# Reordering single steps: the first half's output projection and row norm against the second half's attention and convolution norm

## The chip, the cores and the metric

The kernel runs on one core of a Trainium2 chip. The metric is the device time of one execution in microseconds; lower is better. All data is float32. Matrix products are made three times over (high part by high part, high by low, low by high), each operand being split into a rounded high part and the rest.

## The reference

One hybrid decoder layer on 1024 tokens of 1024 channels. What matters here:

```python
proj = x @ w_in + b_in                       # q 512, k 128, v 128, a 512, gate 512 columns
y_attn = sliding_window_gqa(q, k, v, sinks, rel_bias_table)   # 8 heads, blocks of 128, own and previous block
h = causal_depthwise_conv(a * sigmoid(gate), conv_dw_w, conv_dw_b)      # 31 taps
y_conv = silu(layer_norm(h, conv_ln_g, conv_ln_b))
y = concat([rms_norm(y_attn, attn_out_gain), rms_norm(y_conv, conv_out_gain)])
x = layer_norm(ALPHA * x + y @ w_out + b_out, ln1_g, ln1_b)
h = causal_depthwise_conv(x @ w_up, ffn_dw_w, ffn_dw_b)       # 3 taps, 5632 columns
g, u = split(h)
out = layer_norm(ALPHA * x + (silu(g) * u) @ w_down, ln2_g, ln2_b)
```

## The kernel before

The 1024 tokens are two halves of 512, H = 0 and H = 1, each of four tiles of 128 tokens. Every stage is a Python generator that issues some instructions and yields. A string, `SCRIPT`, says in which order the generators are advanced: one letter, one step. The letters that matter here:

- `o`, `out_proj(0)`: the output projection of the first half, four steps, one for each 256 output columns. A step casts and splits its weights (L231 on ScalarE, L233 on GpSimd), makes 96 matmuls (L638 to L644) and adds them to the residual rows (`acc`, L648 and L650 on VectorE). `O` is the same for the second half.
- `l`, `first_norm` with `ln1(0)`: four steps, one for each token tile: row statistics (L298, L300), the power on GpSimd (L293), three operations on a row of 1024 (L311 VectorE, L312 GpSimd, L313 VectorE), eight transposes (L278), their copies (L281 ScalarE, L282 VectorE). `L` is the same for the second half, to which `other_sums` (L747) adds the block sums that the later product needs.
- `A`, `attn(1)`: the attention of the second half. 16 units (a token tile, a key group, a pair of heads) go through `front` (six score matmuls L505, L510 on VectorE, L517 the exponential on ScalarE, L526 on GpSimd), then one step later `mid` (four transposes L537, a copy L539, a subtraction L540), then one step later `back` (six matmuls L558 to L560; after every fourth unit L565 and L567), and after a tile its sum (L578). That makes 21 steps. `a` is the same for the first half.
- `C`, `conv(1)`: the 31-tap convolution of the second half on VectorE (L421). `N`, `conv_norm(1)`: the norm of its result, three steps: sums on GpSimd (L443, L444), a matmul (L445), subtractions (L449), squares and their sums (L433); then the reciprocal deviation spread by a matmul (L459, L461); then scaling, SiLU and the gains (L466 to L472).
- `f`, `ffn(0, alone)`: the first six of 22 channel groups of the feed-forward part for the first half. Nine steps: up, up, down, three times. An up step is two products of 24 matmuls (L265, L266, L268) with their convolution (L673 to L678) and gate (L691 to L694); a down step is 48 matmuls (L713 to L715), added by L720. It needs all four `l` steps.
- `s`, `first_sums`: sums of the first half's columns. After the script comes `joint`, the rest of the feed-forward part on both halves at once (from L793 on).

The letters set the order in which instructions are written down. A planner then places each engine's instructions by that order and by the time at which it expects their data, so an instruction written later can stand ahead on its engine. Matrix products that were tied together (`chain`), taps and loads keep their written order. On the chip each engine works through its own list in order.

SBUF places are fixed by hand in lanes that several tiles use in turn. Three of these orders matter: the convolution norm of the second half uses lanes 40 to 47, which hold the first half's attention output until `out_proj(0)` has read it; the second half's output projection keeps its weights in lanes 48 to 55, which hold the second half's values (`vpad`) and transposed probabilities (`ph`) until attention's last `back`; and `ln1(0)` writes to lanes 16 to 31, which hold `out_proj(0)`'s weights.

```python
LANES_NORM1 = {'nsum': [44, 45], 'nz': [40], 'nsq': [42, 43, 46, 47]}
LANES_OUT1 = {'bo': [32], 'oh': [48, 49, 50, 51, 52], 'ol': [53, 54, 55, 38, 39], 'or': [34, 36]}
    for k in SCRIPT:
        if k == 'c':
            drain(steps[k])
        else:
            next(steps[k], None)
    drain(*steps.values())
```

Of the kernel before, what the change touches and what calls it, by code (L numbers as in the profile page):

```python
# [33 lines left out]
LINE = 384  # L34
GROUP = 2
ALONE = 6
SCRIPT = ('0hx00j0hxixxiiiggacaaaaaaaaaaaaannnCCaaagagCkCqqaaaqqoAAAoA'
          'AAAAoAAoNAlAlNAlAlNAAAAfAfAAOOOfsOsssffLLLLffff')
SKEW = (1, 2, 5)
KOFF = (4, 5)  # L40
AHEAD = 1
# [28 lines left out]
def hybrid_layer_kernel(  # L70
# [132 lines left out]
    def parameters():  # L203
        tp = psB()
        for i, pr in enumerate((pr1, pr2, pr3)):
            nc.tensor.transpose(out=tp[:, i * P:(i + 1) * P], in_=pr, identity=ident)
        nc.vector.tensor_copy(out=par, in_=tp[:, 0:3 * P].rearrange("p (i c) -> p i c", c=P))
        nc.vector.tensor_scalar(out=bq8, in0=par[:, 0, 0:4], scalar1=-0.125, scalar2=None, op0=ALU.mult)
# [799 lines left out]
    parameters()  # L1008
    for k in SCRIPT:
        if k == 'c':  # L1010
# [63 lines left out]
```

## Time and profile before

| | |
|---|---|
| median of three runs | 1112.66 us (1112.2 to 1114.48) |
| profiled execution | 1113.39 us |
| its span, first to last instruction | 1111.6 us |
| mean granted TensorE clock | 0.981 |
| TensorE matmul busy | 1050.4 us, 94% |
| VectorE busy | 788.9 us, 71% |
| ScalarE busy | 481.9 us, 43% |
| GpSimd busy | 654.5 us, 59% |

A row of the windows view gives, for a stretch of the span, its length, then for each engine the busy time in it and the number of instructions, then the granted TensorE clock and the DMA share. A row of the timeline has start, duration, engine, line, operation, the tiles it writes and reads, and in brackets the engine's idle time before it and what ended that. A row of the groups has busy time and mean nanoseconds, then the idle time before.

### The profile page before, as it was taken

To read this page: it belongs to the slowest core of one execution; us is meant where nothing else is said; L and a number is where in the kernel's file an instruction comes from. 1 tells how busy PE (TensorE), PEld (TensorE's weight loads), DVE (VectorE), ACT (ScalarE), POOL (GpSimd) and SP (SyncE) were. 2 spreads that over 40 slices of the span, in tenths; PEclk is the share of its full clock that TensorE was granted. 3 is DMA by queue.
4 is the path that set the end of the run, shared out by engine and by line. 5 is a ranking of instruction groups with operands and counts; after the bars stand their busy time and mean duration, and the time that the engine had idled before them with its cause. 6 is when DMAs were issued, how large, how long until landed. Compare 5 with 4: busy or idle time off the path is not lost.

```text
span 1111.6 us, 14383 instructions
## 1 busy us (share of the span) xinstructions
PE 1050.4 (94%) x5113; PEld 873.9 (79%) x5113; DVE 788.9 (71%) x1430; ACT 481.9 (43%) x915; POOL 654.5 (59%) x560
## 2 busy tenths in 40 slices
PE   7999999878968999898999999999999999999996
PEld 5887778778957998676788787878788787888875
DVE  2899789999897448985746656564747566569656
ACT  4546677753548333462515242433425142442430
POOL 3749688775587556455736372746556363636551
PEclk9999999999978999899999999999999999999999
DMA  6535221413600242131211021111212110233321
GB/s 183 160 87 132 77 57 40 139 53 98 186 20 1 78 132 65 50 110 43 76 37 59 20 82 32 58 56 38 76 39 76 35 60 20 76 114 115 113 95 75
DMA packets 115641, 85.19 MB, mean 77 GB/s; under 512 B 20354, under 2 KB 108017, under 8 KB 115569
## 3 DMA queue, kind: packets, MB, share of 16 engines
q1 hardware_dynamic: 112368, 78.92, 23.9%
q10 hardware_dynamic: 3201, 5.35, 1.4%
q8 instruction: 40, 0.66, 0.2%
q14 instruction: 32, 0.26, 0.1%
HBM read 80.05 MB, written 4.21 MB: 76 GB/s over the span
## 4 chain that ended last, share of the span: by engine, by line
PE 76%; DVE 13%; DMA 4%; POOL 3%; ACT 3%; issue 1%; SPq 0%; POOLq 0%; DVEq 0%; ACTq 0%
PE psA L265 6%; PE psA L266 6%; PE psA L268 5%; PE psS L713 2%; PE psS L714 2%; PE psS L715 2%; PE psS L796 2%; PE psS L794 2%; PE psS L793 2%; PE psA L794 2%; PE psA L796 2%; PE psA L793 2%; PE psS L505 2%; PE psA L638 1%; PE psA L713 1%
## 5 line engine op out<-in xcount | busy, mean ns | idle before, releaser
L233 POOL TENSOR_TENSOR wl<-raw,wh 128x512 fp32r<-128x512 f32 x196 | 263.3, 1355 | 162.2 <-ACT wh L231 68.9
L231 ACT CAST wh<-raw 128x512 fp32r<-128x512 f32 x196 | 119.1, 620 | 173.5 <-PE psA L266 24.1
L233 POOL TENSOR_TENSOR wl<-ts,wh 128x512 fp32r<-128x512 f32 x64 | 82.5, 1296 | 155.4 <-ACT wh L231 135.5
L421 DVE SCALAR_TENSOR_TENSOR psC<-hconv,const,psC 128x512 f32<-128x512 f32 x196 | 147.3, 751 | 3.5
L265 PE MATMUL psA<-x,wh 128*128 128x512 f32 x336 | 135.9, 404 | 7.9 <-DVE z L678 4.1
L266 PE MATMUL psA<-x,wh 128*128 128x512 f32 x336 | 134.4, 400 | 0.0
L231 ACT CAST wh<-ts 128x512 fp32r<-128x512 f32 x64 | 39.3, 622 | 177.4 <-PE psS L715 39.2
L268 PE MATMUL psA<-x,wl 128*128 128x512 f32 x336 | 87.2, 396 | 0.6 <-POOL wl L233 0.6
L265 PEld LDWEIGHTS psA<-x,wh 128*128 128x128 f32 x336 | 64.9, 193 | 23.9 <-issue 4.7
L266 PEld LDWEIGHTS psA<-x,wh 128*128 128x128 f32 x336 | 64.9, 193 | 13.5 <-issue 0.2
L268 PEld LDWEIGHTS psA<-x,wl 128*128 128x128 f32 x336 | 62.3, 188 | 15.1 <-issue 1.2
L293 POOL TENSOR_TENSOR tiny<-tiny,const 128x1 f32<-128x1 f32 (+1 forms) x28 | 26.5, 951 | 53.7 <-DVE tiny L292 50.7
L720 DVE TENSOR_TENSOR acc<-psS,acc 128x512 f32<-128x512 f32 x52 | 35.7, 688 | 31.4 <-PE psS L715 31.4
L233 POOL TENSOR_TENSOR ol<-or,oh 128x512 fp32r<-128x512 f32 x32 | 40.7, 1296 | 18.9 <-ACT oh L231 16.6
L793 PE MATMUL psA<-x,wh 128*128 128x512 f32 x112 | 43.6, 389 | 0.0
L794 PE MATMUL psA<-x,wh 128*128 128x512 f32 x112 | 43.6, 389 | 0.0
L793 PE MATMUL psS<-x,wh 128*128 128x512 f32 x112 | 43.6, 389 | 0.0
L794 PE MATMUL psS<-x,wh 128*128 128x512 f32 x112 | 43.6, 389 | 0.0
L832 POOL TENSOR_TENSOR ts<-raw,ts 128x512 f32<-128x512 f32 x32 | 42.0, 1313 | 1.3
L413 POOL TENSOR_TENSOR cp<-cp,cp 128x512 f32<-128x512 f32 x28 | 36.0, 1287 | 8.4 <-ACT cp L409 8.4
L713 PE MATMUL psS<-wh,gh 128*128 128x512 f32 x88 | 35.0, 397 | 5.9 <-ACT gh L693 3.1
L638 PE MATMUL psA<-oh,x 128*128 128x256 f32 x128 | 37.9, 296 | 1.9 <-ACT z L399 1.5
(383 smaller groups left out, 3057.9 us busy)
## 6 DMA issues: line engine op xcount, KB each, us to landing
raw<-in_w_up SPq DMA_DIRECT2D x56, 512.0 KB
raw<-in_w_down SPq DMA_DIRECT2D x28, 512.0 KB
raw<-in_w_in SPq DMA_DIRECT2D x20, 512.0 KB
raw<-in_x SPq DMA_DIRECT2D x8, 512.0 KB
raw<-in_w_in SPq DMA_DIRECT2D x16, 256.0 KB
acc<-in_x SPq DMA_DIRECT2D x8, 512.0 KB
or<-in_w_out SPq DMA_DIRECT2D x64, 64.0 KB
or<-in_w_out SPq DMA_DIRECT2D x8, 512.0 KB
```

Of the source, the lines that this page charges most:

```text
L231: nc.scalar.copy(out=h, in_=part)
L233: nc.gpsimd.tensor_tensor(out=l, in0=part, in1=f(h), op=ALU.subtract)
L265: m.append(nc.tensor.matmul(out=o, lhsT=wh[kt], rhs=xh[kt], start=kt == 0, stop=False))
L266: m.append(nc.tensor.matmul(out=o, lhsT=wh[kt], rhs=xl[kt], start=False, stop=False))
L268: m.append(nc.tensor.matmul(out=o, lhsT=wl[kt], rhs=xh[kt], start=False, stop=kt == KT - 1))
L421: tap(nc.vector.scalar_tensor_tensor(out=dst if k == KO else total, in0=src, scalar=cdw(k, c), in1=total, op0=ALU.mult, op1=ALU.add))
L638: m.append(nc.tensor.matmul(out=pa[:, 0, :], lhsT=yah[:, c, :], rhs=wa[0][c], start=c == 0, stop=False))
L713: m.append(nc.tensor.matmul(out=o, lhsT=gh[:, tsl], rhs=wh, start=j == 0, stop=False))
L793: m.append(nc.tensor.matmul(out=o, lhsT=wh[k], rhs=xh[k], start=k == 0, stop=False))
L794: m.append(nc.tensor.matmul(out=o, lhsT=wh[k], rhs=xl[k], start=False, stop=False))
L796: m.append(nc.tensor.matmul(out=o, lhsT=wl[k], rhs=xh[k], start=False, stop=k == 3))
L832: nc.gpsimd.tensor_tensor(out=t, in0=x0, in1=x1, op=ALU.subtract)
```

## The change

Only `SCRIPT` changes. Both strings are the same up to the first `o` and from the first `OOO` on, and hold the same letters; between these the order differs.

```diff
-SCRIPT = ('0hx00j0hxixxiiiggacaaaaaaaaaaaaannnCCaaagagCkCqqaaaqqoAAAoA'
-          'AAAAoAAoNAlAlNAlAlNAAAAfAfAAOOOfsOsssffLLLLffff')
+SCRIPT = ('0hx00j0hxixxiiiggacaaaaaaaaaaaaannnCCaaagagCkCqqaaaqqoAoAoA'
+          'oAAlAlAlNlAANAAAANAAAAfAfAAAOOOfsOsssffLLLLffff')
```

Step by step, with the number of `A` steps that stand before each:

| step | before | after |
|---|---|---|
| second, third, fourth `o` | 3, 8, 10 | 1, 2, 3 |
| four `l` | 11, 12, 13, 14 | 5, 6, 7, 7 |
| three `N` | 10, 12, 14 | 7, 9, 13 |
| first and second `f` | 18, 19 | 17, 18 |
| first `O` | 21 | 21 |

## The prediction

> **What bounds the kernel now.** I read the page's head, the slices and the chain first, then the windows around the changed steps, then single rows of the timeline.
>
> ```profile
> span 1111.6 us, 14383 instructions
> PE   7999999878968999898999999999999999999996
> DVE  2899789999897448985746656564747566569656
> PEclk9999999999978999899999999999999999999999
> PE 76%; DVE 13%; DMA 4%; POOL 3%; ACT 3%; issue 1%; SPq 0%; POOLq 0%; DVEq 0%; ACTq 0%
> ```
>
> TensorE (PE) is nearly full; the time lies in the slices where it is not. One slice is 27.8 us: slice 12 (306 to 333 us) is the deepest hole, with a clock digit of 7, and there VectorE (DVE) is full. The next stretches in windows:
>
> ```profile
> 245.00:308.00 63.00, 59.85 (x462) 55.90 (x461) 58.45 (x148) 29.18 (x86) 37.14 (x46) 1.00 0.41 126
> 308.00:345.00 37.00, 24.71 (x112) 19.69 (x113) 34.46 (x76) 21.42 (x52) 31.64 (x31) 0.68 0.05 15
> 345.00:372.00 27.00, 27.00 (x142) 23.07 (x142) 14.98 (x29) 18.72 (x34) 16.08 (x13) 1.00 0.08 20
> 372.00:429.00 57.00, 57.00 (x434) 55.01 (x433) 30.96 (x62) 14.59 (x25) 29.80 (x26) 1.00 0.37 112
> 429.00:499.00 70.00, 64.33 (x283) 51.61 (x283) 66.01 (x102) 34.83 (x58) 41.20 (x27) 0.95 0.23 69
> 499.00:1111.00 612.00, 590.22 (x2583) 484.81 (x2582) 383.62 (x631) 217.96 (x368) 326.75 (x252) 0.99 0.21 64
> ```
>
> Columns: length, then busy time of PE, its weight loads, DVE, ScalarE (ACT), GpSimd (POOL), then the clock. Which work stands in which stretch is told by these rows:
>
> ```profile
> 305.30 4.56 POOL L443 TENSOR_TENSOR nsum<-cy,cy 128x512 f32<-128x512 f32 x2 [3.54 <-PE psA L640]
> 306.50 0.28 PE L644 MATMUL psA<-oh,x 128*128 128x256 f32 x1
> 309.83 2.34 POOL L312 TENSOR_TENSOR acc<-acc,g 128x1024 f32<-128x1024 f32 x1
> 345.66 0.40 PE L265 MATMUL psA<-x,wh 128*128 128x512 f32 x1
> 368.36 0.28 PE L560 MATMUL psY<-ph,vpad 128*128 128x256 f32 x1
> 368.72 3.80 POOL L233 TENSOR_TENSOR ol<-or,oh 128x512 fp32r<-128x512 f32 x3 [2.27 <-PE psY L560]
> 371.68 0.28 PE L638 MATMUL psA<-oh,x 128*128 128x256 f32 x1
> 428.95 0.40 PE L265 MATMUL psA<-x,wh 128*128 128x512 f32 x1
> 498.84 0.39 PE L793 MATMUL psA<-x,wh 128*128 128x512 f32 x1
> ```
>
> So: the first half's output projection ends at 306.5; the feed-forward part `f` begins at 345.66, when the row norm is through. Between them DVE is busy 34.46 of 37 us (row norm, convolution norm, attention) and PE starves. From 345 to 429 PE is full and DVE half idle. Attention's last `back` ends at 368.6; only then can POOL split the second half's output weights, which go into the lanes of `vpad` and `ph` (the 2.27 us wait for psY), and `O` runs from 371.68 to 428.95. From 429 to 499 DVE is full again (66.01 of 70) with the second row norm and the block sums, and PE waits. After 499 PE has work to the end. Hence two gates: the start of `f`, and the end of attention, behind which `O`, the second row norm and the joint part queue.
>
> **The change part by part.** No instruction is added or removed. No load is moved past another on SP's queue: `A` and `N` load nothing, and `o`, `l`, `f` keep their order. On POOL `N`'s sums move behind the row norm's multiplications. What one attention unit costs:
>
> ```profile
> L510 DVE CUSTOM_DVE_ANT_0 hank<-psS,bias,const 128x256 f32<-128x256 f32 (+1 forms) x64 | 27.4, 458 | 10.8 <-PE psS L505 5.7 <-PE psT L537 3.2 <-PE psA L268 1.7
> L540 DVE TENSOR_TENSOR ph<-psT,ph 128x512 fp32r<-128x512 f32 (+1 forms) x32 | 20.7, 647 | 0.1
> L567 DVE SCALAR_TENSOR_TENSOR x<-psY,const,x 128x128 fp32r<-128x128 f32 x32 | 9.0, 341 | 3.3 <-ACT x L565 3.3
> 306.71 0.97 PE L505 MATMUL psS<-kh,x 64*128 64x256 f32 x6
> 308.53 0.60 PE L537 MATMUL psT<-const,hank 128*128 128x128 f32 x4
> L459 DVE TENSOR_SCALAR nz<-const,tiny 128x128 f32<-128x128 f32 x4 | 1.1, 345 | 0.0
> L433 POOL TENSOR_TENSOR nsq<-nsq,nsq 128x512 f32<-128x512 f32 x3 | 4.7, 1599 | 0.0
> ```
>
> 32 units in all: on DVE 27.4/32 + 20.7/32 + 9.0/32 = 1.78 us. On PE 0.97 + 0.60 and again 0.97 for the six `back` matmuls; their ends overlap, so I take 2.2 of 2.5.
>
> *The start of `f`.* The pace of attention (L540 once a unit):
>
> ```profile
> 204.00:238.00 34.00, 5.45 (x8) 0.97 0.29 86
> 258.00:308.00 50.00, 5.41 (x8) 1.00 0.45 138
> 308.00:345.00 37.00, 3.38 (x5) 0.68 0.05 15
> 345.00:372.00 27.00, 2.04 (x3) 1.00 0.08 20
> L540 DVE TENSOR_TENSOR ph<-psT,ph x3: 678/681/683, 347.6 to 360.6; 128x512 fp32r<-128x512 f32 x3
> ```
>
> Before, 13 units are through L540 at 345. After, the script asks for seven `A` steps ahead of the last `l`, though engines that are free take more; I take 9 units (bounds 7 and 12). Four fewer are 4 x 1.78 = 7.1 us of DVE; the second `N` step goes behind too, 1.1 us (L459). On POOL the sums stood ahead of the row norm: 4.56 (L443), whose head waited 3.54 us for the projection's last read, and 4.7 (L433), 9.3 us; DVE was busy meanwhile, so I credit half, 4.6. Sum 12.8: `f` would start at 332.9 (bounds: three gained with 12 units and no credit, 342; 6 x 1.78 + 1.1 + 9.3 = 21 gained, 325).
>
> *What that is worth to PE.* The four units are 8.8 us of PE work that now lies behind `f`'s start, with about 1 us of `N`'s matmuls: 12.8 - 9.8 = 3.0 us gained. Between the projection and `f` PE now has less to do than in the hole of before, where the clock was 0.68, and `f` may begin on half clock. The row for that:
>
> ```profile
> 459.27 0.76 PE L265 MATMUL psA<-x,wh 128*128 128x512 f32 x1 [3.50 <-DVE z L678]
> 459.83 0.63 PE L266 MATMUL psA<-x,wh 128*128 128x512 f32 x1
> 460.26 0.63 PE L265 MATMUL psA<-x,wh 128*128 128x512 f32 x1
> 345.89 0.40 PE L266 MATMUL psA<-x,wh 128*128 128x512 f32 x1
> ```
>
> After an idle time of 3.50 us matmuls came every 0.43 us, not every 0.23 (345.66 to 345.89). With a dozen such, as an estimate for some 5 us, 12 x 0.2 = 2.4 us are lost (bounds 0 and 4.8): 0.6 us of the gain remain. The Trainium skill ("TensorE: Matmul & The Clock Gate", Part 1) states that the clock falls to half after an idle window of about 3.4 us and comes back after about as much sustained work; the 3.50 us row agrees. By that page a cold start costs half a window, an estimate of 1.7 us, and 1.3 us would remain.
>
> *The end of attention.* Seven units are left at 332.9. Their pace: 34/8 = 4.25 us from 204 to 238, 50/8 = 6.25 from 258 to 308, 7.4 in the hole, 9 at the very end, where ACT held the third `N` step. After 333 DVE has room (14.98 of 27), as it had not in the slower two, so I take 4.25: 7 x 4.25 = 29.8, the last L540 at 362.7. From L540 to the end of the last `back` it was 368.6 - 360.6 = 8.0: 370.7, so 2.1 us later than before. At 6.25 it is 16 us later; with 12 units done by 342 and 4.25 it is 342 + 17 + 8 = 367, 1.6 us earlier. PE does not idle meanwhile: the first `f` steps are four products of 24 x 0.23 = 5.5 us, and a down step follows.
>
> *What of it reaches the end.* `O` starts later by that, and so does the stretch bound by DVE (429 to 499). But the `f` work that was done meanwhile is missing there, on DVE too:
>
> ```profile
> L676 DVE SCALAR_TENSOR_TENSOR z<-psA,const,z 128x511 f32<-128x511 f32 x14 | 10.4, 741 | 1.6 <-ACT z L673 1.6
> L678 DVE SCALAR_TENSOR_TENSOR z<-psA,const,z 128x510 f32<-128x510 f32 x14 | 10.4, 741 | 0.1
> L691 DVE TENSOR_TENSOR z<-z,z 128x512 f32<-128x512 f32 x8 | 8.9, 1119 | 0.2
> L694 DVE TENSOR_TENSOR gl<-z,gh 128x512 fp32r<-128x512 f32 x12 | 10.0, 834 | 7.3 <-ACT gh L693 7.3
> ```
>
> A product needs 0.74 + 0.74 + (1.12 + 0.83)/2 = 2.46 us of DVE for 5.5 us of PE, 0.45. The joint part starts later by the delay less 0.45 x (delay + gain): 2.1 - 0.45 x (2.1 + 0.6) = +0.9 us. Against the profiled 1113.39 (1.8 us above its span, 0.7 above the median) that is 1114.3; against the median 1113.5. A measurement of this kernel tells about 0.2%, 2.2 us, from no change.
>
> **The rivals.** *Slower:* with `f`'s casts, its convolution and the late `N` steps on ACT and POOL beside it, attention keeps the pace of 258 to 308, 6.25 us. The delay is 16, the time +16 - 0.45 x 16.6 = +8.5: 1121. For it speaks 9 us per unit after 345 with DVE half idle; against it, that only three units stood there, beside ACT's burst. It decides when the last `back` ends after about 374.
>
> *Faster:* the row norm is a chain with waits of its own (DVE to POOL and back), and attention fills its gaps on DVE, now that the convolution norm's sums are out of POOL's way. Then 11 units are done when `f` starts: 2 x 1.78 + 1.1 + 4.6 = 9.3 us earlier, at 336.4. Five are left, the last `back` ends at 336.4 + 21.2 + 8.0 = 365.6, 3.0 earlier. PE is given 9.3 - 5.4 - 2.4 = 1.5 us; the time is -3.0 + 0.45 x (3.0 - 1.5) = -2.3. With POOL's 9.3 us credited in full `f` starts at 331.7, attention ends 7.7 earlier, PE is given 6.2, and it is -7.7 + 0.45 x 1.5 = -7.0. Between the two: 1108. For it speaks POOL's 31.64 of 37 us in the hole; against it, DVE's 34.46. It decides when the last `back` ends before 366.
>
> *The change doesn't do what it says:* the planner places by readiness, and attention already stood behind the script at 308 (8 units through where ten steps were asked before the last `o`). Then the engines' lists hardly differ, and the time is that of before, 1112.7.
>
> **How the numbers follow.** My forecast, no measurable change, 0.26 with a time of 1113.5 (own range 1110 to 1117); the planner's lists nearly the same, 0.10; attention late, 0.32; attention early, 0.32. Of the first two together 0.25 lie within 0.2%, 0.05 below and 0.06 above; so faster 0.37, same 0.25, slower 0.38. The range: below, 12 units done and POOL's 9.3 us in full (`f` at 333.5, the last `back` 10.1 earlier, 6.6 given to PE), -10.1 + 0.45 x 3.5 = -8.5, 1104; above, pace 6.25 and the full 4.8 us of cold clock, 1123. I take 1104 to 1123, which leaves a tenth out on each side.
>
> **What the profile after would show.** The last matmul of the first half's projection some 10 us before 306.5; `f`'s first L265 near 333 with matmuls 0.43 us apart; nsum behind the third L312 on POOL; nine units through L540 by then; the last `back` near 371; DVE full before L793, which comes near 500. Wrong would be the step on pace if the last `back` stands beyond 374 or before 366, the step on `f`'s start if it lies outside 325 to 342, and the step on what is given back if the joint part moves by as much as attention's end does.

## The result, and the profile after

| | before | after |
|---|---|---|
| median | 1111.51 us (1110.76 to 1116.28, 10 runs) | 1120.8 us (1116.5 to 1122.93, 10 runs) |
| profiled execution | 1113.39 us | 1121.74 us |

The changed order is slower: ratio 1.0075, 95% interval 1.0063 to 1.0087; the two medians lie 9.3 us apart. Of the page of the kernel after, the span, two lines of the slices and one of the chain:

```profile
span 1119.9 us, 14373 instructions
DVE  2899789989996548995756656574747566569656
PEclk9999999999967999899999999999999999999999
PE 71%; DVE 16%; ACT 4%; DMA 3%; POOL 3%; issue 2%; SPq 0%; POOLq 0%; DVEq 0%; ACTq 0%
```

The chain of waits has 5 points less of PE and 3 more of DVE, and the hole in the clock (digits 6 and 7 in slices 12 and 13, where before had 7 and 8) has grown. The windows of the kernel after, cut at the same events as those of before (end of the first half's projection, `f`, `O`, the second row norm, the joint part; at `O` the cut is where its matmuls run on, behind a single one at 375.60):

```profile
303.00:346.60 43.60, 29.05 (x133) 22.63 (x131) 40.51 (x85) 24.87 (x59) 28.91 (x25) 0.66 0.06 18
346.60:377.50 30.90, 30.19 (x143) 24.42 (x143) 14.70 (x27) 18.46 (x30) 15.28 (x16) 0.92 0.00 1
377.50:435.00 57.50, 57.46 (x434) 55.47 (x435) 32.42 (x65) 15.79 (x29) 33.82 (x29) 1.00 0.40 120
435.00:504.82 69.82, 64.18 (x282) 51.36 (x280) 66.25 (x101) 34.94 (x59) 40.89 (x27) 0.95 0.23 69
504.82:1119.00 614.18, 592.03 (x2584) 486.22 (x2582) 383.68 (x631) 217.97 (x368) 327.13 (x252) 0.99 0.21 64
```

The projection ends at 303.0, 3.8 us earlier than before, and `f` begins at 346.60, 0.9 later: the hole between them is 43.6 us, not 39. `O` and the second row norm have kept their lengths (57.5 and 69.8 us); they are only later. The joint part starts 6.0 us later, and 2.3 more come behind it (last section).

In the hole two things stand out. First, VectorE and GpSimd just behind the projection, after and then before (timeline; L623 is the four operations on the *second* half's residual rows, which its projection needs only from 377.5 on):

```profile
300.32 1.21 DVE L623 SCALAR_TENSOR_TENSOR acc<-acc,bo 128x1024 f32<-128x1024 f32 x1
301.63 3.51 POOL L443 TENSOR_TENSOR nsum<-cy,cy 128x512 f32<-128x512 f32 x2 [1.20 <-PE psA L640]
301.91 2.09 DVE L623 SCALAR_TENSOR_TENSOR acc<-acc,bo 128x1024 f32<-128x1024 f32 x1
303.93 1.77 DVE L311 TENSOR_SCALAR acc<-acc,tiny 128x1024 f32<-128x1024 f32 x1
305.61 1.21 DVE L623 SCALAR_TENSOR_TENSOR acc<-acc,bo 128x1024 f32<-128x1024 f32 x1
305.77 3.25 POOL L312 TENSOR_TENSOR acc<-acc,g 128x1024 f32<-128x1024 f32 x1 [0.63 <-DVE acc L311]
308.19 1.92 DVE L623 SCALAR_TENSOR_TENSOR acc<-acc,bo 128x1024 f32<-128x1024 f32 x1
308.99 2.25 POOL L444 TENSOR_TENSOR nsum<-nsum,nsum 128x512 f32<-128x512 f32 x1
310.84 0.68 DVE L540 TENSOR_TENSOR ph<-psT,ph 128x512 fp32r<-128x512 f32 x1
311.29 2.07 PE L445 MATMUL psN<-nsum,const 128*128 128x512 f32 x2 [5.94 <-POOL nsum L444]
```

```profile
299.45 1.23 DVE L623 SCALAR_TENSOR_TENSOR acc<-acc,bo 128x1024 f32<-128x1024 f32 x1 [0.40 <-DMA acc<-in_x]
301.64 1.21 DVE L623 SCALAR_TENSOR_TENSOR acc<-acc,bo 128x1024 f32<-128x1024 f32 x1
305.29 1.21 DVE L623 SCALAR_TENSOR_TENSOR acc<-acc,bo 128x1024 f32<-128x1024 f32 x1
306.42 0.68 DVE L540 TENSOR_TENSOR ph<-psT,ph 128x512 fp32r<-128x512 f32 x1
307.42 1.32 DVE L623 SCALAR_TENSOR_TENSOR acc<-acc,bo 128x1024 f32<-128x1024 f32 x1
```

Before, three of the four are through when the projection ends, and the last one stands behind attention's eighth unit (L540): 4.97 us in all. After, all four stand ahead of that unit and take 6.43 us, the 1.21 us of L623 growing to 2.09 and 1.92; nsum is still ahead of the row norm's L312 on GpSimd, where the change had written it behind. The eighth unit, 0.4 us before the projection's end there, is 7.8 us behind it here.

Second, ScalarE around the start of `f` (timeline, after):

```profile
339.89 1.28 ACT L467 ACT_TABLE_LOAD   x1
346.44 0.82 ACT L467 ACTIVATE cy<-cy,const 128x512 f32<-128x512 f32 x1
347.28 1.28 ACT L521 ACT_TABLE_LOAD   x1
348.57 0.20 ACT L521 ACTIVATE tiny<-tiny 128x4 f32<-128x4 f32 x1
349.81 0.57 ACT L281 CAST x<-psA 128x512 fp32r<-128x512 f32 x1
357.99 1.28 ACT L689 ACT_TABLE_LOAD   x1 [1.71 <-DVE z L678]
```

The convolution norm's four SiLU (L467) stand ahead of attention's last exponential (L521) and of the row norm's last copy (L281), with two table loads more than before.

### The profile page after: what moved, and what is told of

It is laid out like the page before. It is cut to its first block, busy times and chain, and to the rows that moved or that the text cites. A ratio compares the mean times of both kernels' runs of the same rounds, so it can differ in the third digit from the quotient of the medians.

```text
span 1119.9 us, 14373 instructions
## 1 busy us (share of the span) xinstructions
PE 1056.4 (94%) x5113; PEld 877.1 (78%) x5113; DVE 796.1 (71%) x1430; ACT 484.5 (43%) x917; POOL 654.1 (58%) x560
## 4 chain that ended last, share of the span: by engine, by line
PE 71%; DVE 16%; ACT 4%; DMA 3%; POOL 3%; issue 2%; SPq 0%; POOLq 0%; DVEq 0%; ACTq 0%
PE psA L265 5%; PE psA L266 5%; PE psA L268 5%; PE psS L713 2%; PE psS L714 2%; PE psS L715 2%; DVE psC L421 2%; PE psS L796 2%; PE psS L794 2%; PE psS L793 2%; PE psA L794 2%; PE psA L796 2%; PE psA L793 2%; PE psS L505 1%; PE psA L713 1%
## 5 line engine op out<-in xcount | busy, mean ns | idle before, releaser
L293 POOL TENSOR_TENSOR tiny<-tiny,const 128x1 f32<-128x1 f32 (+1 forms) x28 | 23.0, 826 | 60.8 <-DVE tiny L292 57.7
L793 PE MATMUL psA<-x,wh 128*128 128x512 f32 x112 | 43.6, 389 | 0.0
L794 PE MATMUL psA<-x,wh 128*128 128x512 f32 x112 | 43.6, 389 | 0.0
L793 PE MATMUL psS<-x,wh 128*128 128x512 f32 x112 | 43.6, 389 | 0.0
L794 PE MATMUL psS<-x,wh 128*128 128x512 f32 x112 | 43.6, 389 | 0.0
```

The source lines that it names most:

```text
L793: m.append(nc.tensor.matmul(out=o, lhsT=wh[k], rhs=xh[k], start=k == 0, stop=False))
L794: m.append(nc.tensor.matmul(out=o, lhsT=wh[k], rhs=xl[k], start=False, stop=False))
```

## The experiments

Names of the program's lines shift by up to 17 in the kernels with edits inside functions. `follow(i, x)` places operation `i` behind `x` on its engine's list. The part of the order from the first `o` to the first `OOO`:

```
before              oAAAoAAAAAoAAoNAlAlNAlAlNAAAAfAfAA
after               oAoAoAoAAlAlAlNlAANAAAANAAAAfAfAAA
e1_o_only           oAoAoAoAAAAAAANAlAlNAlAlNAAAAfAfAA
e5, e6, e8, e9      oAoAoAoAAlAlAlNlAANAAAAAAAANfAfAAA
g2, g3              oAAAoAAAAAoAAoAlAlAlAlNAANANfAfAAA
h3                  oAAAoAAAAAoAAoAlAlNAlNAlNAAAAfAfAA
h4                  oAoAoAoAAAAAAAAlAlNAlNAlNAAAAfAfAA
```

What all gave: ratio to before with its interval; then from each one's profiled execution the events, in us behind the first matmul of the first half's projection (217.53 before, 216.35 after; it differs by up to 2.8 us between the profiled executions), and the length from the joint part's start to the end. `O` is its first matmul; in seven of the kernels this one stands alone, ahead of the last `back`, and the others follow behind that.

| | ratio | `f` | last `back` ends | `O` | joint | joint to end |
|---|---|---|---|---|---|---|
| before | 1 | 128.1 | 151.1 | 154.1 | 281.3 | 612.8 |
| after | 1.0075 [1.0063, 1.0087] | 130.3 | 160.4 | 159.2 | 288.5 | 615.1 |
| e1_o_only | 1.0072 [1.0052, 1.0092] | 125.9 | 158.1 | 156.9 | 285.7 | 617.7 |
| e5_silu_behind | 1.0026 [1.0015, 1.0038] | 127.8 | 156.9 | 155.8 | 284.1 | 612.9 |
| e6_mids_first | 1.0059 [1.0042, 1.0075] | 130.3 | 159.0 | 160.2 | 287.0 | 612.7 |
| e8_both | 1.0023 [1.0011, 1.0035] | 126.8 | 154.3 | 155.5 | 282.4 | 615.7 |
| g1_rows | 0.9941 [0.9920, 0.9962] | 119.3 | 149.3 | 148.1 | 276.6 | 613.4 |
| g2_sums | 1.0031 [1.0014, 1.0048] | 119.6 | 146.2 | 148.1 | 282.9 | 617.9 |
| g3_rows_sums | 1.0035 [1.0017, 1.0052] | 114.5 | 144.1 | 143.0 | 284.0 | 613.2 |
| e9_all | 0.9977 [0.9957, 0.9997] | 119.9 | 151.8 | 151.7 | 280.1 | 616.6 |
| h1_o_rows | 0.9936 [0.9913, 0.9958] | 118.3 | 147.6 | 146.3 | 275.0 | 612.6 |
| h2_after_rows | 0.9959 [0.9946, 0.9972] | 118.9 | 152.6 | 151.5 | 280.1 | 610.9 |
| h3_rows_sums2 | 0.9925 [0.9905, 0.9945] | 115.0 | 143.0 | 142.8 | 271.8 | 617.3 |
| h4_o_rows_sums2 | 0.9972 [0.9952, 0.9991] | 117.3 | 149.3 | 149.1 | 277.3 | 612.4 |

**Which part of the order costs.** `N` alone has no run: with only `N`'s letters moved in the order of before (as far as they stay behind the last `o`), every engine's list comes out as before, and with only `N`'s letters moved back in the changed order, as in the kernel after. That leaves `o` and `l`; `l` alone has no run either.

> One part alone: only the second to fourth o steps are moved ahead; l, N and f keep their place behind ten A steps, as before. On ScalarE's list the third N step's SiLU then stands behind the last row norm copies and behind attention's last exponential, without the two further table loads (1.28 us each) that the changed kernel had at 347.3 and 358.0 us. Theory 1 (the loss of 9 us comes from what stands ahead of the last row norm copy and of attention's last units on the in-order lists): f starts some 3 us earlier than at 346.6, the second half's output projection about 374, ratio to before about 1.004. Theory 2 (the loss is the early o steps themselves, which hold attention back on TensorE and VectorE from 245 us on): the whole loss stays, 1.0075. Theory 3 (f merely starts on half clock, 2.8 us): 1.0075 less nothing, as the hole is the same.

The whole loss is there with the `o` steps alone, 1.0072, the size that theory 2 gave, though `f` now starts 2.3 us earlier than before: it doesn't come through `f`'s start. Attention's last `back` ends 7.0 us later than before (158.1 against 151.1) and the joint part starts 4.4 us later. Another 4.9 us of this profiled execution lie behind the joint part's start, in its clock (last section).

**What stands ahead of `f`'s start and attention's last units.** e5 puts the SiLU behind the last exponential and the last row-norm copy, e6 puts `f`'s products 2, 3, 4 behind the transposes of the last three units, which in the kernel after stand behind 48, 71 and 93 of `f`'s matmuls; e8 does both. All three also have the third `N` step written just ahead of `f`.

```diff
 # e5
+ i = nc.scalar.activation(out=y[c], ..., func=AF.Silu, ...)
+ if H == 1: follow(i, last exponential, last row-norm copy)
 # e6
+ first = mm3(p, *w, xh, xl)
+ if H == 0 and k in (1, 2, 3): follow(first, transposes of unit 13 + k)
```

> The changed order (with the third N step written just ahead of f), and the four SiLU of that step placed on ScalarE's list behind attention's last exponential and behind the last row norm copy. Theory 1: two table loads fewer (2.6 us) and copies that no longer wait behind SiLU: f starts about 343 instead of 346.6, the output projection of the second half about 374 instead of 377.5, ratio 1.004 to 1.005. Theory 2: 1.0075. Theory 3: 1.0075.

> The changed order (third N step as in the run before), and f's second, third and fourth products placed on TensorE's list behind the transposes of attention's 14th, 15th and 16th unit, which in the changed kernel stood behind 48, 71 and 93 of f's matmuls. Theory 1: attention's last matmul ends near 371 instead of 376.8, the projection starts some 5 us earlier, ratio about 1.003. Theory 2: the transposes' data come no earlier, TensorE waits instead, 1.007 to 1.010.

> Both placements of the two runs before together. Theory 1: the projection of the second half starts within 2 us of 371.7, ratio 0.999 to 1.002. Theory 2: 1.006 or more. If theory 1 holds only for one of the two placements, this equals the better of the single ones.

The SiLU gives 0.5% back, the transposes 0.16%, which is not told from nothing (the intervals of e6 and of the kernel after overlap), both 0.52%: one table load is left, and `f` comes 3.5 us earlier in e8. Theory 1 had asked for more of the transposes (1.003). ScalarE's rows in e5 (timeline), where the copies now stand ahead of the one load:

```profile
343.01 0.59 ACT L288 CAST x<-psA 128x512 fp32r<-128x512 f32 x1 [0.86 <-PE psA L285]
343.87 0.59 ACT L288 CAST x<-psA 128x512 fp32r<-128x512 f32 x1 [0.16 <-PE psA L285]
345.42 1.28 ACT L474 ACT_TABLE_LOAD   x1
```

But the eighth unit is still 4.1 us later in e8 than before, counted from the first matmul (5.6 in the kernel after), and e1, where the SiLU makes one load only, lost as much as the whole change. So these two were not the root.

**The residual rows and the sums.** On the order of *before*, g1 moves the four L623 behind the row norm, g2 moves nsum behind it (what the change was said to do; `N`'s letters go behind the last `l` as well), g3 both.

```diff
 # g1
+ i = nc.vector.scalar_tensor_tensor(out=a, in0=a, scalar=ALPHA, in1=bo, ...)
+ if H == 1: follow(i, last row-norm subtraction of the first half)
 # g2
+ first = nc.gpsimd.tensor_tensor(out=sums[i], in0=y[2 * i], in1=y[2 * i + 1], op=ALU.add)
+ if H == 1: follow(first, last row-norm multiplication of the first half)
```

> The order of before, unchanged; only the four operations on the second half's residual rows (L623, 1.21 to 2.09 us each on VectorE, needed only when its output projection ends) stand behind the first half's last row-norm operation. Theory A (the lists of VectorE between the first projection's end and the start of f gate both f and attention): some 5 us leave a stretch where VectorE is busy 34.46 of 37 us, so f starts 3 to 5 us earlier than 128.2 us behind the first matmul of the second-half-weights lane order, that is behind the first output projection's first matmul, attention's end moves by as much, and the time falls by 3 to 4 us: ratio 0.9965 (0.994 to 0.999). Theory B (PE's total work behind the projection decides, what is gained at f's start is given back in the next stretch bound by VectorE): the four operations cost the same there, ratio 1.000 within 0.001.

> The order of before, with the convolution norm's three steps written behind the last step of the row norm and its first two sums on GpSimd (L443, 4.56 us for the two, the first waiting 3.54 us) placed behind the row norm's last multiplication there. This is the one thing that the change was said to do and that the lists after it do not have. The prediction's term (half of GpSimd's 9.3 us of sums, 4.6, comes off f's start): f 4 to 5 us earlier, and the time lower by as much if attention's end goes with it, ratio 0.996 to 0.998. Rival: VectorE, not GpSimd, held the row norm, so f gains 0 to 1 us; and the convolution norm, now 10 us or more later, brings its SiLU and squares behind f's start, so attention or the second output projection waits for them: ratio 1.001 to 1.005.

> Both of the two edits before on the order of before. If the two gates are separate, the differences add: f 7 to 9 us earlier and the ratio 0.993 to 0.995 by theory A with the prediction's term; 0.9965 if only VectorE's rows count; if VectorE was the gate that hid GpSimd's sums, together they give more than the two alone. Theory B: within 0.002 of 1.000.

> The order of after with the third step of the convolution norm just ahead of f, all four SiLU behind attention's last exponential and the last row-norm copy, the products of f placed behind the transposes of the last three units (these edits together left 1.0023 of 1.0075), and the four residual-row operations of the second half behind the row norm. In the trace of after these four stand on VectorE ahead of attention's unit 8 (6.4 us). Theory A: unit 8 and all behind it come 4 to 6 us earlier, the joint part 3 to 4 us, and the order of after becomes as fast as before or a little faster: ratio 0.998 to 1.000. Theory B: the early output projection itself costs the remaining 0.0023, and the rows make no difference: 1.002 to 1.003.

g1 is 0.59% faster than before, more than expected: `f` starts 8.8 us earlier, and the joint part 4.7. But g1 isn't the rows alone. Its rows on GpSimd (timeline):

```profile
301.62 2.40 POOL L320 TENSOR_TENSOR acc<-acc,g 128x1024 f32<-128x1024 f32 x1 [1.36 <-DVE acc L319]
304.57 2.54 POOL L451 TENSOR_TENSOR nsum<-cy,cy 128x512 f32<-128x512 f32 x2 [0.56 <-PE psA L650]
```

Before, the row norm's first multiplication began at 309.83, behind nsum; with the rows away the planner puts it ahead of nsum, 8.2 us earlier. What the rows do with nsum left in front is seen in e9 and in h1 and h2 below, where nsum stays ahead as in the kernels that they are compared with.

g2 moves `f` by nearly as much as g1, 8.5 us, and is slower: in the rival's range, though the rival had given `f` 1 us at most. g3, 1.0035, falls into none of the cases written for it. Windows from `O`'s start to its end, g2 and then g3, and in g3 TensorE's waits in it and ScalarE's first late SiLU:

```profile
364.90:430.20 65.30, 61.24 (x444) 58.15 (x443) 37.69 (x70) 19.58 (x37) 37.73 (x31) 0.97 0.33 100
```

```profile
361.50:431.80 70.30, 63.52 (x442) 60.08 (x443) 38.92 (x75) 23.45 (x43) 40.18 (x34) 0.93 0.33 98
```

```profile
361.13 0.80 ACT L477 ACTIVATE cy<-cy,const 128x512 f32<-128x512 f32 x1
365.55 0.39 PE L654 MATMUL psA<-oh,x 128*128 128x256 f32 x1 [0.93 <-ACT x L478]
367.32 0.50 PE L656 MATMUL psA<-oh,x 128*128 128x256 f32 x2 [1.04 <-DVE x L479]
376.43 1.86 PE L443 MATMUL psN<-const,nsq 128*128 128x1 f32 x8 [2.19 <-POOL nsq L441]
```

`O` takes 65 and 70 us instead of 57: it reads the convolution norm's result, which now comes as `O` starts, and TensorE waits in the middle of it, then for its squares, and loses clock. What `f` gained is spent there. e9 shows that the rest of the loss in e8 goes with the rows and not with the early projection: 1.0023 becomes 0.9977.

**The rows on the changed order.** h1 is e1 with g1's edit, h2 the kernel after with g1's edit; h3 is g1 with nsum behind the *second* row-norm multiplication (and the first two `N` letters later), h4 h3 with the early `o` steps.

> The four early out_proj(0) steps of the change alone (the rest in the order of before), with the second half's residual rows behind the row norm. It differs from g1_rows in the place of the o steps only, as e1_o_only (1.0072) differs from before. If the early projection costs through attention's first units, which are left behind on TensorE while it runs, the loss is the same with the rows out of the way: 0.9941 + 0.0072 = 1.001 (1.000 to 1.003). If in e1 it cost through the rows, which stood on VectorE ahead of unit 8, nothing of it is left: 0.994 to 0.996.

> The changed order as it is, with that one edit: the second half's four residual-row operations behind the row norm's last. If the rows are a cost of their own, the same in both orders (0.0059 on the order of before), the ratio to before is 1.0075 - 0.0059 = 1.0016 (1.000 to 1.003). If the SiLU on ScalarE and the table loads ahead of the last row-norm copies gate f in the changed order, f gains little by the rows, and it is 1.004 to 1.007.

> g1_rows with the convolution norm's first two sums on GpSimd behind the second of the four row-norm multiplications there, not behind the fourth as in g3_rows_sums (1.0035, where f started 5 us earlier than in g1_rows, and the second half's output projection then waited for the convolution norm). If that wait is the price of a norm 18 us late, half of the delay is free: f 1 to 3 us earlier than in g1_rows, the projection's 57.8 us unchanged, ratio 0.992 to 0.994. If any delay of the norm shifts its SiLU and squares into the time of f's first products, the projection takes longer and the ratio is 0.995 to 1.000.

> The early out_proj(0) steps of the change, with the rows behind the row norm and the sums behind its second multiplication on GpSimd: h3_rows_sums2 (0.9925) with the o steps moved. If the early projection is neutral once VectorE is free of the rows (h1_o_rows 0.9936 beside g1_rows 0.9941), this is h3 again: 0.991 to 0.994, f some 115 us behind the first output projection's first matmul as in h3. If the row norm now starts earlier with the projection, what the change was read as doing, f comes 2 to 4 us earlier and the ratio is 0.988 to 0.991. If the early projection leaves attention's units behind, 0.995 to 0.998.

h1 at 0.9936 and g1 at 0.9941: with the rows out of the way the early `o` steps cost nothing that shows, where with them they had cost 0.72%. h2 takes the changed order from 1.0075 to 0.9959, twice what the rows gave on the order of before, and past it; both cases written for it had 1.000 or more. With the rows out, the two orders (g1 and h2) lie 0.18% apart and their intervals overlap, where with the rows in it was 0.75%. Its rows (timeline), beside those of the kernel after above:

```profile
301.67 2.55 POOL L451 TENSOR_TENSOR nsum<-cy,cy 128x512 f32<-128x512 f32 x2 [1.87 <-PE psA L650]
304.17 2.40 POOL L320 TENSOR_TENSOR acc<-acc,g 128x1024 f32<-128x1024 f32 x1
304.40 0.64 DVE L548 TENSOR_TENSOR ph<-psT,ph 128x512 fp32r<-128x512 f32 x1
307.02 1.29 POOL L452 TENSOR_TENSOR nsum<-nsum,nsum 128x512 f32<-128x512 f32 x1
334.76 1.09 ACT L288 CAST x<-psA 128x512 fp32r<-128x512 f32 x2
335.42 0.57 PE L272 MATMUL psA<-x,wh 128*128 128x512 f32 x1
337.80 1.28 ACT L475 ACT_TABLE_LOAD   x1
339.55 4.62 DVE L631 SCALAR_TENSOR_TENSOR acc<-acc,bo 128x1024 f32<-128x1024 f32 x4
```

nsum 2.55 instead of 3.51 us, the row norm's multiplication 2.40 instead of 3.25, nsum is ready at 308.31 instead of 311.24; the eighth unit (L548 here) 6.4 us earlier; the four rows later take 4.62 us together, with GpSimd idle beside the first three; and one table load stands behind the last copies, although nothing was done to the SiLU here. So the edits of e5 and e6 mended what comes only with the rows: with the rows out they bring nothing (e9 0.9977, h2 0.9959, intervals overlapping).

h3 is the fastest, 0.9925 [0.9905, 0.9945]: half the delay of nsum is free, `O` takes 59.4 us. It beats both kernels, as g1, h1, h2, h4 and e9 do, though it isn't told apart from g1 and h1. h4 falls to the third case written for it: the early `o` steps on h3 cost 0.5%, `f` and the joint part coming 2.4 and 5.5 us later. TensorE then idled once for 5.0 us on an attention unit; which placement ahead of it did that is open. The early projection is thus free in one arrangement of the lists and dear in two.

What this doesn't settle: each edit also makes the planner place other operations anew, so 1.2% is the price of where the rows stand, with all that follows from it in the lists, and not of 6.4 us of VectorE alone. A run with every other place kept fixed wasn't made, nor one with the rows out on the order of before and nsum kept in front.

## Why the prediction was right or wrong

The time, 1120.8, lies in the range, but that is luck: it is 7.3 us above the forecast, which was no measurable change, and the change is slower beyond the noise. It is the time of the rival "slower" (1121), reached by another sum. Step by step:

**The start of `f` failed.** Forecast 332.9 (bounds 325 and 342), measured 346.60. Two terms of it fell. The four units that were to wait behind `f`: twelve were through L540 by then, not nine, for the planner places by readiness. The sums on GpSimd: they did not move, nsum stands at 301.63 ahead of the first L312. The text had the third rival's reason in hand (eight units through where ten steps were asked) and gave it 0.10; for `N` it was the whole truth. And a term was missing: L623, three quarters through before when the projection ends, and in the changed order 6.43 us of VectorE at the head of the hole, ahead of the eighth unit.

**The credit for GpSimd's sums was too small, and its price was missing.** 4.6 of 9.3 us was taken; with `N` really moved (g2), `f` came 8.5 us earlier. But whoever waits for `N` was not named: `O` grew by 7.9 us.

**The projection's end,** forecast some 10 us earlier, came 3.8 earlier: four `o` steps standing closer still share TensorE with attention (197 other matmuls run within the projection, before 213).

**The cold clock held.** 2.4 us were taken (0 to 4.8). `f`'s first 48 matmuls took 13.7 us, where 0.23 us each makes 11.0: 2.7 lost.

**The pace of attention failed.** 4.25 us a unit was taken for the seven units left. Only four were left, and they took 7.1 us each: the last L540 came at 374.95, not 362.7. That is the rival "slower" in kind, even beyond its 6.25. Part of it is the place of transposes and SiLU in the lists: with both edits (e8) the same four take 5.4 us each. It is not the rows, for with them out (h2) the four take 7.9. What makes up the rest is open. The forecast of the last `back`, 370.7 against a measured 376.8, was the sum of errors that partly cancel: its last term, 8.0 us from the last L540 to the end of the last `back`, measured 1.8. What the rows do to attention they do earlier: with them out, the eighth unit comes 6.7 us earlier against the first matmul, the last `back` 7.8.

**What is given back was sized and placed wrongly.** 0.45 of the delay and the gain was to return behind `O`, by `f` work that is missing there. From `O`'s end to the joint part it is 69.7 us before and 69.9 after, and 69.4 to 70.3 in the other twelve kernels, so nothing returns there: in all of them the same 96 matmuls of `f`'s up steps run ahead of `O` and one down step of 48 within it. What did return lies ahead of `O`: attention's end moved by 8.2 us and the joint part by 6.0, because before TensorE had 3.0 us of `f` to do between the last `back` and `O`, and after it had none left there. So 2.2 us returned where the rule, 0.45 x (8.2 - 0.9), has 3.3.

The sum's last part was right in kind: the delay with which `O` runs on (377.5 against 371.7) reaches the joint part in full.

## What to carry to other kernels

Before a step is moved earlier, list what else becomes ready in the stretch it moves into: work with far due times (here rows needed some 70 us later) is taken by a planner that goes by readiness, and on an engine in fixed order it delays everything behind it. Push such work behind the critical chain first; only then is a change of order worth timing, since the same early `o` steps cost 0.72% with the rows in the hole and nothing that shows with them gone (though 0.5% once more when nsum was moved too, h4). And when a step is moved later, name its reader: moving `N` gave `f` 8.5 us and took them back at `O`.

## What the runs showed of the hardware

**VectorE and GpSimd slow each other.** L623 takes 1.21 us, and 2.09 and 1.92 when it begins beside a running GpSimd operation; L311 takes 0.80 us (before), and 1.77. On GpSimd the two L443 take 2.55 us together (h2), and 3.51 and 4.56 (after, before) with such rows beside them, L312 2.40 and 3.25. In the kernel after, each of these operations that begins within one of the other engine takes about its own time and what is left of the other one, as if they took turns: L623 at 301.91 begins while the first L443 has 1.01 us to go, and 1.21 + 1.01 = 2.22 (measured 2.09); L312 begins while L623 has 1.05 us to go, and 2.40 + 1.05 = 3.45 (measured 3.25). The first one is not slowed: L623 at 305.61 took 1.21 us, the first L443 1.29. The Trainium skill ("SBUF — State Buffer", Who interferes with whom) states that a VectorE instruction with two SBUF inputs contends with a GpSimd instruction that reads SBUF, and that the order of issue decides who blocks. The trace agrees for L623, which reads two rows; L311, which reads one, is slowed too.

**About half a window of idle time on TensorE costs the next window half its clock.** Behind the joint part's start the kernels do the same work, yet take 610.9 to 617.9 us. Gaps at a few places make it, each followed by full clock in some kernels and by half clock in others. Two of them, with the window around each: the kernels before and after at the first, then the kernel after and h3 at the second:

```profile
678.74 0.50 PE L713 MATMUL psS<-wh,gh 128*128 128x512 f32 x1 [1.67 <-ACT gh L817]
670.00:700.00 30.00, 28.33 (x126) 23.12 (x125) 19.93 (x33) 7.52 (x14) 11.78 (x10) 1.00 0.06 18
```

```profile
685.38 0.50 PE L713 MATMUL psS<-wh,gh 128*128 128x512 f32 x1 [2.34 <-ACT gh L817]
676.00:706.00 30.00, 27.66 (x116) 22.39 (x115) 18.82 (x32) 7.18 (x13) 9.86 (x8) 0.94 0.06 18
1085.27 0.50 PE L713 MATMUL psS<-dh,gh 128*128 128x512 f32 x1 [1.91 <-ACT gh L693]
1066.00:1106.00 40.00, 38.09 (x168) 31.25 (x167) 26.20 (x39) 9.30 (x16) 16.72 (x14) 1.00 0.24 84
```

```profile
1069.49 0.50 PE L725 MATMUL psS<-dh,gh 128*128 128x512 f32 x1 [1.84 <-ACT gh L705]
1050.00:1090.00 40.00, 38.16 (x161) 31.09 (x161) 24.51 (x36) 9.29 (x16) 16.43 (x13) 0.96 0.25 88
```

1.91 us passed at full clock (1.00), 1.84 us did not (0.96). The slow stretches in the records run at half clock, are 3.41 us long or a multiple of it, and within a trace all begin a whole number of 3.41 us apart: the clock goes by fixed windows. The gap of 1.84 us (1067.65 to 1069.49) lies within one of them (1066.74 to 1070.15), and the next is slow; that of 1.91 us is cut by a border at 1085.14, into 1.77 and 0.14. So it goes behind 500 us in all 14 traces: all 31 windows at full clock with 1.84 us of idle time or more were followed by a slow one, and none of the 2427 with up to 1.77; of three between, two were. The time behind the joint part's start follows the count: 610.9 us with no slow window but that at the very end (h2), 612.4 to 613.2 with one, 617.3 to 617.9 with four, some 1.7 us for each, half a window. The Trainium skill ("TensorE: Matmul & The Clock Gate", What's actually happening) calls the window free-running, and the trace agrees; an idle time of a whole window, which it asks for, was not needed here, where about half did.

So of the 8.3 us between the two profiled spans, the 2.3 behind the joint part's start are one slow window more (1.7) and the longer gap (0.7), and single executions of these kernels can differ by some us for this alone; how much of the medians' 9.3 us comes from there is open.
